# A decoder trunk on one Trainium2 core: the first stage written out in a fixed order, with column sums of squares on TensorE, weight folding on ScalarE and x loaded from two queues

## The chip, the cores and the metric

The kernel runs on one core of a Trainium2 chip. The core has five engines with a queue of instructions each: PE (TensorE, matrix products), ACT (ScalarE), DVE (VectorE), POOL (GpSimd) and SP (SyncE, which here only starts transfers). Each engine works through its own queue in order and waits at an instruction until what it needs is there. Transfers between the chip's memory and the core run on 16 DMA engines that are started from a queue.

The metric is the device time of one execution in microseconds (us), as the median of several runs. Times inside an execution are read from a profile of one execution, counted from the start of its span.

## What is computed

A trunk of two decoder layers over 1024 tokens of width 1024, all in float32. Cut to the part that matters here:

```python
h = x
for l in range(DEPTH):                       # 2 layers
    u = rmsnorm(h, attn_norm[l])             # u = h * rsqrt(mean(h*h) + eps) * g
    proj = u @ w_in[l]
    rq, rk, rv, rg, dq, dk, dv = jnp.split(proj, offsets, axis=-1)
    ret = retention_chunkwise(rq, rk, rv)    # 4 heads, gated by silu(rg)
    dif = diff_attention(dq, dk, dv, lam)    # 4 heads, two softmaxes subtracted, causal, ALiBi
    h = h + jnp.concatenate([ret, dif], -1) @ w_out[l]
    u = rmsnorm(h, ffn_norm[l])
    h = h + (jax.nn.silu(u @ w_gate[l]) * (u @ w_up[l])) @ w_down[l]
return rmsnorm(h, final_norm)
```

Only the beginning is touched by the change: the first `rmsnorm` on `x` and the first three products that follow it, which are `dk`, `dq` and `dv` of attention heads 0 and 1.

## The kernel before

The activations lie transposed: `h` is eight tiles `h[k]` of 128 channels x 1024 tokens, `k` = 0 to 7, and every step works on the two halves of 512 tokens. In the profile these tiles are called `a`. A product over the 1024 channels is a sum over `k` in one PSUM bank. To keep float32 precision at a higher rate, nearly every operand is split in two fp32r parts, `hi` (a cast on ACT) and `lo` (the difference, on DVE or POOL), and a product is three matmuls: hi times hi, hi times lo, lo times hi (`mm3`, and the same in `tm_pair`).

The first stage of the program, in the order in which `run` writes it:

- **Loads.** All from SP's queue: half of the first weight tile (`wr`), four `x` tiles of half 0, the other half of the weight, four more `x` tiles, the second weight tile (L1202, L1198), then the eight tiles of half 1, then two weight tiles for the values.
- **First products, early.** The K and Q products of head 0 for half 0 don't wait for the norm. The weights are multiplied by the norm's gains on DVE (L1205, into `fold`, called `sp` in the profile), plain float32 matmuls of the folded weights with raw `h` run on PE (`fm_first`, L289), and the result is scaled later by the norm's factor per token (L674).
- **Norm of half 0.** ACT squares each `h[k]` (L408), DVE adds the eight squares into `acc` (L415), PE sums `acc` over the channels with four tiny matmuls against a column of ones (L380, a *column sum*), a few 128x4 instructions on DVE and ACT turn this into the factor y (L385 to L392, L346, L389), and PE spreads y over the partitions by four transposes (L396). Then for each `k`: DVE multiplies `h[k]` by gain and y (L428), ACT casts it to `hi` (L430), and DVE, for two of the eight POOL, makes `lo` (L432).
- **Norm of half 1.** The same, with its squares and adds laid between the steps of half 0.
- **Values** of half 0 (`tm_pair`, L305 to L307): 96 matmuls of 128x256, then K, Q and values of half 1 (`fm_half`, L270 to L272, then L305 to L307), interleaved with the first attention scores (L556, L557).

What sets the order: for PE the order is as written, everywhere. For ACT, DVE, POOL and SP a scheduler orders the instructions by priorities, except in the feed-forward part, which is also written out by hand. `weave` interleaves two generators in a fixed proportion. Buffers come from pools of a fixed number of tiles (for example three `wr`, five `t`, two `kb`), and an instruction that writes a buffer waits until the last reader of its former content is done.

Of the kernel before, what the change touches and what calls it, by code (L numbers as in the profile page):

```python
# [146 lines left out]
class Trunk:  # L147
# [41 lines left out]
    def late_consts(self):  # L189
        nc, a = self.nc, self.a  # L190
        nc.sync.dma_start(self.tabs, a["tabs"])
# [92 lines left out]
    def fm_first(self, h, ws):  # L284

        for w in ws:
            ps = self.bank("mm")
            for k in range(KT):
                self.nc.tensor.matmul(ps, lhsT=w[:, P * k:P * k + P], rhs=h[k][:, 0:HT], start=k == 0,  # L289
                                      stop=k == KT - 1)  # L290
                yield 4
            self.first_ps.append(ps)

# [78 lines left out]

    def rsqrt_rows(self, parts, dim, cols=HT, gap=14):
        nc = self.nc
        nt = cols // P
        x = self.t("nx", 2, [P, 4])[:, :nt]
        banks = [self.bank(t) for t in (("s", "s", "t", "t")[:nt] if len(parts) > 1 else ("s",))]
        for i, sq in enumerate(parts):
            for t in range(nt):
                nc.tensor.matmul(banks[t % len(banks)][:, t:t + 1], lhsT=sq[:, P * t:P * t + P],  # L380
                                 rhs=self.ones[:, 0:1].bitcast(F32), start=i == 0, stop=i == len(parts) - 1)
# [11 lines left out]
        yield gap  # L393
# [4 lines left out]
        return out[:, :cols]  # L398

    def squares(self, h, sl, alone, kb=False, first=False):  # L400
# [4 lines left out]
        for k in range(KT):  # L405
            s = (tmp() if k else self.t("acc", 2, [P, 512]))[:, :n]
            with nullcontext() if first else self.tc.high_priority():
# [10 lines left out]
    def norm_half(self, h, hf, gcol, us, lag=11, gap=9, first=False, keep=False):  # L418
        nc = self.nc
        sl = slice(hf * HT, hf * HT + HT)  # L420
        parts = self.squares(h, sl, 0, True, first)
# [4 lines left out]
        for k in range(KT):  # L426
# [4 lines left out]
            eng = nc.gpsimd if keep and k in (1, 4) else nc.vector  # L431
            eng.tensor_tensor(out=lo[:, k], in0=f, in1=hi[:, k].bitcast(F32), op=ALU.subtract)  # L432
        if keep:
            self.first_y = self.big("sp")[:, 0:HT]
            nc.scalar.copy(self.first_y, y)
# [229 lines left out]
    def attention(self, l, us, w_first, norm1):  # L665
        wk, wq, wdv = w_first
        nc = self.nc
        v, qk, outs = {}, self.qk_tiles(), []
        kq = lambda hf: self.chain(self.stacks(wk, us, (hf,), qk[1], 1.0), self.stacks(wq, us, (hf,), qk[0], 0.125))
        first = [self.chain(kq(hf), self.values(wdv, us, hf, v)) for hf in range(NH)]  # L670
        if l == 0:
            for ps, st, scale in zip(self.first_ps, (qk[1], qk[0]), (1.0, 0.125)):
                f = self.tmp()
                nc.vector.tensor_tensor(out=f, in0=ps, in1=self.first_y, op=ALU.mult)  # L674
                self.stack(f, st, slice(0, HT), scale)
            self.weave(norm1, 40, self.values(wdv, us, 0, v), 48)
            self.late_consts()
        else:
            self.weave(norm1, 96, first[0], 96)
        self.prev, self.norms, self.outs = None, [], []  # L680
        for h in range(4):
# [7 lines left out]
            if h == 0:  # L689
                self.weave(self.att_part(l, A, 0, 4), PART0, first[1], 96)  # L690
# [416 lines left out]
    def layer(self, l, h, us, w_first, norm1, after):  # L1107
# [7 lines left out]
        o_out, rq, rk = self.attention(l, us, w_first, norm1)  # L1115
# [72 lines left out]
    def run(self):  # L1188
        nc = self.nc
        self.nf = 0  # L1190
        h = [self.big("a4") for _ in range(KT)]
        raws = [self.big("wr") for _ in range(2)]
        fold = [self.big("sp") for _ in range(2)]

        def load(hf, ks):
            sl = slice(hf * HT, hf * HT + HT)
            for k in ks:
                nc.sync.dma_start(h[k][:, sl], self.a["xT"][k][:, sl])  # L1198

        def load_w(i, c):  # L1200
            cs = slice(512 * c, 512 * c + 512)
            nc.sync.dma_start(raws[i][:, cs], self.a["wts"][i][:, cs])  # L1202
# [60 lines left out]
```

## Time and profile before

| what | value |
|---|---|
| median of 3 runs | 2310.18 us (2310.01, 2310.18, 2485.22) |
| profiled execution, its own time | 2310.15 us |
| span of the profiled execution | 2308.4 us |
| PE busy over the span | 2263.9 us (98%) |
| DVE, ACT, POOL busy | 1393.8, 1010.4, 762.4 us |
| first matmul of the first stage | 5.52 us |
| first matmul of half 1's K product | 46.30 us |
| first matmul of half 1's values | 59.60 us |

How to read it: the profiled execution's own time is 1.75 us above its span, and 0.03 us from the median. A busy PE is not a PE at its peak: the table of stretches has a column with the TensorE clock that was granted (1.00 is full speed), and the distance from the start of one matmul to the start of the next tells the real rate. A float32 matmul of 128x512 or 128x1 is recorded as two matmul instructions (called *passes* below), so the 16 matmuls of `fm_first` are 32 records.

### The profile page before, as it was taken

The page shows a single profiled execution, that of the slowest core. Times are in us where ns is not written, and L with a number is a line of the kernel's source. Part 1 is how long each engine was busy: PE and PEld are TensorE (multiplying, and loading weights), DVE is VectorE, ACT ScalarE, POOL GpSimd, SP SyncE. Part 2 cuts the span into 40 slices and gives each one's busy share as a digit, 9 for nine tenths or more (in the row PEclk, how much of TensorE's full clock was granted, in tenths as well). Part 3 has the DMA queues.
Part 4 walks back from the last instruction along what each step waited for, and adds up shares of the span by engine and source line. Part 5 has one row for each costly group of instructions (what it writes and reads, how often), then busy time and mean ns, then how long its engine had stood idle before and what let it go on. Part 6 is the DMA issues. An engine that isn't in the chain of part 4 may idle for free.

```text
span 2308.4 us, 30689 instructions
## 1 busy us (share of the span) xinstructions
PE 2263.9 (98%) x11328; PEld 1898.0 (82%) x11328; DVE 1393.8 (60%) x2576; ACT 1010.4 (44%) x1905; POOL 762.4 (33%) x608
## 2 busy tenths in 40 slices
PE   7999999999999999999999999999999999999998
PEld 5888898787788888888888888988878888888887
DVE  8777612987534333895567775059874443359856
ACT  5666533444333333543256665234443333344332
POOL 3111212122444455336121112211235444544350
PEclk9999999999999999999999999999999999999999
DMA  5212131111332322752232222112123232345422
GB/s 165 76 47 65 38 100 38 56 55 55 128 120 88 118 100 92 233 182 93 69 106 55 56 65 81 57 37 74 53 90 119 82 124 83 108 157 194 162 65 73
DMA packets 74214, 216.58 MB, mean 94 GB/s; under 512 B 8016, under 2 KB 10064, under 8 KB 74064
## 3 DMA queue, kind: packets, MB, share of 16 engines
q1 hardware_dynamic: 74064, 214.62, 28.8%
q8 instruction: 89, 1.46, 0.3%
q14 instruction: 61, 0.50, 0.1%
HBM read 162.16 MB, written 44.04 MB: 89 GB/s over the span
## 4 chain that ended last, share of the span: by engine, by line
PE 79%; DVE 11%; ACT 3%; issue 2%; DMA 2%; POOL 1%; DVEq 0%; SPq 0%; POOLq 0%; ACTq 0%
PE ps_mm L246 8%; PE ps_mm L247 7%; PE ps_mm L248 7%; PE ps_mm L271 6%; PE ps_mm L272 6%; PE ps_mm L270 6%; PE ps_s L246 4%; PE ps_s L247 4%; PE ps_s L248 4%; PE ps_t L246 3%; PE ps_t L247 3%; PE ps_t L248 3%; PE ps_mm L307 2%; PE ps_mm L305 2%; PE ps_mm L306 2%
## 5 line engine op out<-in xcount | busy, mean ns | idle before, releaser
L223 POOL TENSOR_TENSOR w<-wr,w 128x512 fp32r<-128x512 f32 x278 | 389.3, 1413 | 469.0 <-ACT w L222 433.9
L263 POOL TENSOR_TENSOR w<-wr,w 128x512 fp32r<-128x512 f32 x140 | 185.2, 1329 | 572.7 <-ACT w L262 537.6
L270 PE MATMUL ps_mm<-u,w 128*128 128x512 f32 (+1 forms) x735 | 296.0, 403 | 0.0
L271 PE MATMUL ps_mm<-u,w 128*128 128x512 f32 (+1 forms) x735 | 287.2, 391 | 2.0 <-DVE u L432 2.0
L272 PE MATMUL ps_mm<-u,w 128*128 128x512 f32 (+1 forms) x735 | 287.3, 391 | 0.0
L222 ACT CAST w<-wr 128x512 fp32r<-128x512 f32 x312 | 187.9, 619 | 142.3 <-DVE wr L889 86.5
L246 PE MATMUL ps_mm<-u,w 128*128 128x512 f32 x432 | 168.6, 390 | 0.0
L247 PE MATMUL ps_mm<-u,w 128*128 128x512 f32 x432 | 168.3, 390 | 0.0
L248 PE MATMUL ps_mm<-u,w 128*128 128x512 f32 x432 | 168.2, 389 | 0.0
L272 PEld LDWEIGHTS ps_mm<-u,w 128*128 128x128 f32 x735 | 138.0, 188 | 30.4
L271 PEld LDWEIGHTS ps_mm<-u,w 128*128 128x128 f32 x735 | 138.3, 188 | 26.1 <-DVE u L432 2.8
L270 PEld LDWEIGHTS ps_mm<-u,w 128*128 128x128 f32 x735 | 138.2, 188 | 23.9
L938 ACT COPY t<-ps_mm 128x512 f32<-128x512 f32 x76 | 44.7, 588 | 246.8 <-PE ps_mm L248 246.7
L262 ACT CAST w<-wr 128x512 fp32r<-128x512 f32 x140 | 85.7, 619 | 133.6 <-PE ps_mm L271 42.6
L305 PE MATMUL ps_mm<-w,u 128*128 128x256 f32 x448 | 128.5, 287 | 0.0
L306 PE MATMUL ps_mm<-w,u 128*128 128x256 f32 x448 | 127.7, 285 | 0.2 <-POOL w L263 0.2
L307 PE MATMUL ps_mm<-w,u 128*128 128x256 f32 x448 | 127.6, 285 | 0.0
L559 DVE CUSTOM_DVE_ANT_0 sp<-ps_s,wr 128x512 f32<-128x512 f32 (+2 forms) x192 | 103.2, 551 | 35.0 <-PE ps_s L557 33.8
L223 POOL TENSOR_TENSOR w<-t,w 128x512 fp32r<-128x512 f32 x52 | 74.9, 1440 | 146.6 <-ACT w L222 146.6
L563 ACT ACTIVATE sp<-sp,m 128x256 f32<-128x256 f32 (+7 forms) x128 | 99.1, 774 | 52.0 <-DVE m L562 51.3
L246 PE MATMUL ps_t<-u,w 128*128 128x512 f32 x288 | 114.0, 396 | 4.8 <-ACT t L938 4.8
L847 DVE TENSOR_TENSOR a<-a,ps_mm 128x512 f32<-128x512 f32 (+1 forms) x148 | 98.6, 666 | 33.1 <-PE ps_mm L248 19.5
(386 smaller groups left out, 5878.0 us busy)
## 6 DMA issues: line engine op xcount, KB each, us to landing
wr<-wts SPq DMA_DIRECT2D x190, 512.0 KB, 3.7
mx<-s_fast SPq DMA_DIRECT2D x56, 512.0 KB, 4.9
s_fast<-mx SPq DMA_DIRECT2D x48, 512.0 KB, 5.0
kb<-ka SPq DMA_DIRECT2D x64, 128.0 KB, 2.3
s_rest<-mx SPq DMA_DIRECT2D x12, 512.0 KB, 2.9
kb<-wts SPq DMA_DIRECT2D x12, 512.0 KB, 5.6
mx<-s_rest SPq DMA_DIRECT2D x12, 512.0 KB, 3.7
a<-xT SPq DMA_DIRECT2D x16, 256.0 KB, 5.4
```

The lines of the kernel that those rows point to most:

```text
L222: nc.scalar.copy(h, src)
L223: (eng or nc.gpsimd).tensor_tensor(out=o, in0=src, in1=h.bitcast(F32), op=ALU.subtract)
L246: mm(ps, lhsT=wh[:, c], rhs=bh, start=first and i == 0, stop=False, skip_group_check=True)
L247: mm(ps, lhsT=wh[:, c], rhs=bl, start=False, stop=False, skip_group_check=True)
L248: mm(ps, lhsT=wl[:, c], rhs=bh, start=False, stop=i == 3, skip_group_check=True)
L263: nc.gpsimd.tensor_tensor(out=o, in0=raw[:, cols], in1=h.bitcast(F32), op=ALU.subtract)
L270: mm(out, lhsT=lh, rhs=rh, start=first, stop=False)
L271: mm(out, lhsT=lh, rhs=rl, start=False, stop=False)
L272: mm(out, lhsT=ll, rhs=rh, start=False, stop=last)
L305: mm(o, lhsT=uh, rhs=wh, start=k == 0, stop=False)
L306: mm(o, lhsT=uh, rhs=wl, start=False, stop=False)
L307: mm(o, lhsT=ul, rhs=wh, start=False, stop=k == KT - 1)
```

## The change

The first stage becomes one function, `start`, whose instructions run on ACT, DVE, POOL and SP in the order in which they are written; the scheduler orders the rest of the program as before. Within it:

- `x` of half 0 comes from two queues: the odd `k` are started from ACT's queue, the even from SP's.
- The second weight tile (i = 1) is multiplied by the gains on ACT, in eight pieces of 128x128, instead of DVE.
- The squares of half 1 are not added up on DVE. Each goes to PE, where four column sums per square accumulate over the eight squares in four PSUM banks. They stand in PE's queue between the fourth and the fifth matmul of the Q product.
- The squares of half 1 and the splits of the value weights are laid between the steps of half 0's norm; the low parts of these weights move from POOL to DVE, two low parts of half 0's norm as well. The K weights' low parts stay on POOL, the Q weights' low parts go to DVE during the norm of half 1.
- The value weights are loaded into `mx` tiles instead of `wr`; `tabs` is loaded here.
- The values of half 0 are issued while the norm of half 1 is written, with all of the PE work of half 0 ahead of them.

```diff
+    def column_sums(self, banks, sq, nt, first, last):
+        for t in range(nt):
+            self.nc.tensor.matmul(banks[t % len(banks)][:, t:t + 1], lhsT=sq[:, P * t:P * t + P],
+                                  rhs=self.ones[:, 0:1].bitcast(F32), start=first, stop=last)
...
-        first = [self.chain(kq(hf), self.values(wdv, us, hf, v)) for hf in range(NH)]
-        if l == 0:
-            for ps, st, scale in zip(self.first_ps, (qk[1], qk[0]), (1.0, 0.125)):
-                f = self.tmp()
-                nc.vector.tensor_tensor(out=f, in0=ps, in1=self.first_y, op=ALU.mult)
-                self.stack(f, st, slice(0, HT), scale)
-            self.weave(norm1, 40, self.values(wdv, us, 0, v), 48)
+        part = lambda hf: self.chain(kq(hf), self.values(wdv, us, hf, v))
+        if begun:
             self.late_consts()
...
+    def start(self, us):
...
+        def fold_w(i, c):
+            if i == 0:
+                g = self.gains[:, 4 * c:4 * c + 4].rearrange("p (k o) -> p k o", o=1).broadcast_to([P, 4, P])
+                blocks = lambda t: halves(t)[c].rearrange("p (k m) -> p k m", m=P)
+                v(out=blocks(fold[i]), in0=blocks(raws[i]), in1=g, op=ALU.mult)
+                return
+            for k in range(4 * c, 4 * c + 4):
+                cs = slice(P * k, P * k + P)
+                nc.scalar.mul(fold[i][:, cs], raws[i][:, cs], self.gains[:, k:k + 1])
...
+        def norm(hf, y, n, beside=lambda k: None):
+            hi, lo = self.t("u", 4, [P, KT, HT], R32), self.t("u", 4, [P, KT, HT], R32)
+            us[hf] = (hi, lo)
+            fs = {}
+            for k in range(KT + 1):
+                if k < KT:
+                    fs[k] = self.tmp()
+                    mul(out=fs[k], in0=h[k][:, hf * HT:hf * HT + HT], scalar=self.gains[:, k:k + 1], in1=y,
+                        op0=ALU.mult, op1=ALU.mult)
+                    cast(hi[:, k], fs[k])
+                if k:
+                    low(lo[:, k - 1], fs.pop(k - 1), hi[:, k - 1])
+                beside(k)
...
+        load_w(0, 0)
+        for k in (1, 3, 5, 7):
+            load(0, k, nc.scalar)
+        load(0, 0)
+        load(0, 2)
+        load_w(0, 1)
+        load(0, 4)
+        load(0, 6)
+        load_w(1, 0)
+        load_w(1, 1)
+        for k in r:
+            load(1, k)
...
+        for k in r:
+            sq = room[k % 4] if k else acc
+            nc.scalar.activation(sq, h[k][:, 0:HT], AF.Square)
+            if k:
+                v(out=acc, in0=acc, in1=sq, op=ALU.add)
+            if k == 2:
+                fold_w(0, 1)
+            if k in (1, 4):
+                split(w_kq[0], raws[0], k // 4)(nc.gpsimd)
+            fm(0, k)
+
+        fold_w(1, 0)
+        bank = [self.bank("s")]
+        self.column_sums(bank, acc, 4, True, True)
+        y = self.rsqrt_small(bank, D, 4)
+        for k in range(4):
+            fm(1, k)
+        y = self.rows(y, 4)
...
+        def square(k):
+            nc.scalar.activation(parts[k], h[k][:, HT:T], AF.Square)
+            self.column_sums(banks, parts[k], 4, k == 0, k == KT - 1)
+        square(0)
...
+        norm(0, y, 0, beside0)
+        for k in range(4, KT):
+            fm(1, k)
+        y1 = self.rsqrt_small(banks, D, 4)
+        keep = self.big("sp")[:, 0:HT]
+        nc.scalar.copy(keep, y)
+        y1 = self.rows(y1, 4)
...
+        first(0)
+        values = self.values(wdv, us, 0, v0)
...
+        norm(1, y1, 1, beside1)
+        self.drain(values)
...
+        with self.tc.manual_schedule(engines={e.Activation, e.DVE, e.Pool, e.SP}):
+            h, w_first, begun = self.start(us)
```

Two places show what the new order is. The first is PE's queue behind the first eight matmuls. The names: `ps_mm` is the product's bank, `a` the raw x, `sp` a folded weight, `c_ones` the ones of a column sum, `c_ident` the identity of the transposes, `ny` the norm's factor. Before:

```order
L289 MATMUL ps_mm_127<-a_6_81,sp_86 128x512
L380 MATMUL ps_s_135<-c_ones,acc_104 128x1 x4
L289 MATMUL ps_mm_127<-a_7_82,sp_86 128x512
L289 MATMUL ps_mm_127<-a_8_83,sp_86 128x512
L289 MATMUL ps_mm_180<-a_1_76,sp_87 128x512
L289 MATMUL ps_mm_180<-a_2_77,sp_87 128x512
L396 MATMUL ps_s_183<-c_ident,ny_141 128x128 x4
L289 MATMUL ps_mm_180<-a_3_78,sp_87 128x512
...
L289 MATMUL ps_mm_180<-a_8_83,sp_87 128x512
L380 MATMUL ps_s_281<-c_ones,acc_155 128x1 x4
L305 MATMUL ps_mm_295<-w_248,u_188 128x256
```

And now (of the 32 column sums of half 1, four for each of the squares in `kb` and `v` tiles, the first and the last are shown):

```order
L364 MATMUL ps_s_157<-c_ones,acc_118 128x1 x4
L1210 MATMUL ps_mm_116<-a_1_78,sp_89 128x512
...
L1210 MATMUL ps_mm_116<-a_4_81,sp_89 128x512
L396 MATMUL ps_s_174<-c_ident,ny_164 128x128 x4
L364 MATMUL ps_s_183<-c_ones,kb_179 128x1
...
L364 MATMUL ps_o_186<-c_ones,v_182 128x1
L1210 MATMUL ps_mm_116<-a_5_82,sp_89 128x512
...
L1210 MATMUL ps_mm_116<-a_8_85,sp_89 128x512
L396 MATMUL ps_s_296<-c_ident,ny_288 128x128 x4
L294 MATMUL ps_mm_322<-w_244,u_194 128x256
```

Half 0's transposes (the first L396) stood behind ten of the sixteen long matmuls and now stand behind twelve; the column sums of half 1, the last four long matmuls and half 1's transposes all stand ahead of the first value matmul (L305, now L294), where before half 1's transposes stood in the middle of the values.

The second place is DVE's queue behind the transposes of half 0. The names: `t` and `u` are a step's product and its low part, `acc` the sum of squares, `w` a low part of a value weight. Before:

```order
L428 SCALAR_TENSOR_TENSOR t_37_190<-a_1_76,c_gains,ps_s_183 128x512
L415 TENSOR_TENSOR acc_155<-acc_155,kb_166 128x512
L428 SCALAR_TENSOR_TENSOR t_38_194<-a_2_77,c_gains,ps_s_183 128x512
L415 TENSOR_TENSOR acc_155<-acc_155,kb_169 128x512
L432 TENSOR_TENSOR u_189<-t_37_190,u_188 128x512
L415 TENSOR_TENSOR acc_155<-acc_155,kb_172 128x512
```

And now:

```order
L1225 SCALAR_TENSOR_TENSOR t_40_196<-a_1_78,c_gains,ps_s_174 128x512
L1225 SCALAR_TENSOR_TENSOR t_41_204<-a_2_79,c_gains,ps_s_174 128x512
L1216 TENSOR_TENSOR u_195<-t_40_196,u_194 128x512
L1225 SCALAR_TENSOR_TENSOR t_42_217<-a_3_80,c_gains,ps_s_174 128x512
L1216 TENSOR_TENSOR u_195<-t_41_204,u_194 128x512
...
L1216 TENSOR_TENSOR u_195<-t_44_235,u_194 128x512
L1216 TENSOR_TENSOR w_245<-mx_110,w_244 128x512
```

The adds of half 1's squares are gone from between the steps of half 0, and four low parts of value weights came in further down. Behind the first stage PE's queue is the same instruction for instruction, 10734 rows up to the end.

More of the change, by code (lines that the diff above doesn't have):

```diff
@@ L1 @@
 import math
[L2 removed]
+from contextlib import ExitStack
 import numpy as np
@@ L397, in rsqrt_rows, with squares @@
                                 identity=self.ident)
-        return out[:, :cols]
-    def squares(self, h, sl, alone, kb=False, first=False):
+        return out
+    def squares(self, h, sl, alone, kb=False):
         nc = self.nc
@@ new lines, in start @@
+        fold_w(0, 0)
+        acc = self.t("acc", 2, [P, 512])
+        room = [x for _ in range(2) for x in halves(self.big("ka"))]
+        for k in r:
[8 more added lines that the diff above has]
+            fm(0, k)
```

153 lines of the change are left out of this document (87 added, 66 removed).

## Prediction, made before the changed kernel was run

> **What bounds the kernel now.** The page first.
>
> ```profile
> span 2308.4 us, 30689 instructions
> PE 2263.9 (98%) x11328; PEld 1898.0 (82%) x11328; DVE 1393.8 (60%) x2576; ACT 1010.4 (44%) x1905; POOL 762.4 (33%) x608
> PE 79%; DVE 11%; ACT 3%; issue 2%; DMA 2%; POOL 1%; DVEq 0%; SPq 0%; POOLq 0%; ACTq 0%
> ```
>
> TensorE is busy 98% of the span and holds 79% of the chain that ended last. The change touches the first 60 us of it, 2.6%. Behind the first stage PE's queue is row for row the same, so I take one instant as the meeting point of both programs: M, the start of the first value matmul of half 1. What M gains or loses, the program gains or loses, unless something behind it had slack; with PE at 98% I assume none. PE's timeline before M:
>
> ```profile
> 37.68 0.41 PE L305 MATMUL ps_mm<-w,u 128*128 128x256 f32 x1
> 37.90 0.41 PE L306 MATMUL ps_mm<-w,u 128*128 128x256 f32 x1
> ...
> 38.67 0.60 PE L396 MATMUL ps_s<-c_ident,ny 128*128 128x128 f32 x4
> ...
> 46.06 0.28 PE L306 MATMUL ps_mm<-mx,u 128*128 128x256 f32 x1
> 46.18 0.28 PE L307 MATMUL ps_mm<-mx,u 128*128 128x256 f32 x1
> 46.30 0.40 PE L270 MATMUL ps_mm<-u,w 128*128 128x512 f32 x1
> ...
> 51.95 0.50 PE L271 MATMUL ps_mm<-u,w 128*128 128x512 f32 x1 [0.89 <-DVE u L432]
> ...
> 59.60 0.28 PE L305 MATMUL ps_mm<-w,u 128*128 128x256 f32 x1
> ```
>
> M is 59.60. From half 1's first matmul at 46.30 to M are 13.30 us with one wait of 0.89 for a low part of u, so 12.4 us without it. A value matmul comes every 0.22 us at 37.68 and every 0.12 us at 46.06: the same instruction at half and at full clock. Which stretches run at half clock the table of stretches tells (columns: length; busy us of PE, PE's weight loads, DVE, ACT, POOL; granted clock; DMA share; GB/s):
>
> ```profile
> 24.00:26.00 2.00, 0.90 (x3) 0.07 (x1) 2.00 (x4) 1.79 (x4) 2.00 (x1) 1.00 0.00 0
> 26.00:28.00 2.00, 1.23 (x10) 1.26 (x11) 2.00 (x3) 1.92 (x4) 2.00 (x3) 1.00 0.00 0
> 28.00:30.00 2.00, 1.78 (x9) 1.49 (x8) 2.00 (x4) 0.62 (x1) 2.00 (x2) 0.51 0.00 0
> ...
> 36.00:38.00 2.00, 2.00 (x11) 2.00 (x11) 1.90 (x5) 1.50 (x4) 0.00 (x0) 0.50 0.17 36
> 38.00:40.00 2.00, 2.00 (x18) 2.00 (x18) 1.12 (x5) 0.00 (x0) 0.00 (x0) 0.93 0.99 210
> ```
>
> The clock is halved from about 28 to 38. The cause is in PE's earlier timeline:
>
> ```profile
> 5.52 8.09 PE L289 MATMUL ps_mm<-a,sp 128*128 128x512 f32 x12 [5.52 <-DMA a<-xT]
> 14.53 1.05 PE L380 MATMUL ps_s<-c_ones,acc 128*128 128x1 f32 x8 [0.92 <-DVE acc L415]
> 15.45 3.68 PE L289 MATMUL ps_mm<-a,sp 128*128 128x512 f32 x8
> 19.12 0.62 PE L396 MATMUL ps_s<-c_ident,ny 128*128 128x128 f32 x4
> 19.58 5.32 PE L289 MATMUL ps_mm<-a,sp 128*128 128x512 f32 x12
> 26.77 1.02 PE L380 MATMUL ps_s<-c_ones,acc 128*128 128x1 f32 x8 [1.88 <-DVE acc L415]
> ```
>
> PE ran dense until 24.9, waited 1.88 us for half 1's sum of squares, did 1.02 us of column sums, and at 28 the clock fell. It came back at about 38.2, after work without a pause since this row (it waited for a low part that POOL made):
>
> ```profile
> 34.10 0.58 PE L307 MATMUL ps_mm<-mx,u 128*128 128x256 f32 x1 [2.32 <-POOL u L432]
> ```
>
> So the return took 4.1 us of dense work.
>
> **The change part by part.** *Half 0's factor.* Its transposes start at 19.12, behind 20 passes. They now stand behind 24, at 5.32/12 = 0.44 us each at full clock 1.8 us more; the wait of 0.92 us for the column sum goes, since two more products stand ahead of it: 19.12 + 1.8 - 0.9 = 20.0. Folding the second weight leaves DVE, where it made half 0's factor late:
>
> ```profile
> 14.39 3.44 DVE L1205 TENSOR_TENSOR sp<-wr,c_gains 128x512 f32<-128x512 f32 x2
> 17.76 0.15 DVE L385 TENSOR_SCALAR nx<-ps_s 128x4 f32<-128x4 f32 x1
> ...
> 39.31 2.07 DVE L428 SCALAR_TENSOR_TENSOR t<-a,c_gains,ps_s 128x512 f32<-128x512 f32 x3 [0.82 <-PE ps_s L396]
> ...
> 42.84 1.90 DVE L432 TENSOR_TENSOR u<-t,u 128x512 fp32r<-128x512 f32 x3
> ```
>
> The column sum was there at about 15.5 and DVE took it at 17.76, two us later. That gain is now covered by the four extra passes on PE: the factor is ready earlier, the transposes are not. If PE were ahead, the gain would show.
>
> *Half 0's steps on DVE.* First multiply 39.31 - 38.67 = 0.64 us after the start of the transposes: 20.6. Then eight multiplies at 2.07/3 = 0.69, and eight low parts and four low parts of value weights at 1.90/3 = 0.63: 13.1 us, until 33.7. POOL's two low parts are gone. ACT beside it:
>
> ```profile
> 18.29 1.13 ACT L408 ACTIVATE kb<-a 128x512 f32<-128x512 f32 x2
> ...
> 55.96 0.40 ACT L636 ACTIVATE sp<-sp,z 128x128 f32<-128x128 f32 x1
> ```
>
> 19 casts and squares at 1.13/2 = 0.57 and four weight pieces. ACT's multiply by a column per partition on 128x128 is in the trace (0.40), so the eight pieces cost 3.2 us, half of them here: 10.8 + 1.6 = 12.4 us, just under DVE's 13.1. The other half lies behind the squares of half 0, in ACT's time before the column sum. Both are hidden; uncovered, a piece would cost 0.4.
>
> *x from two queues.*
>
> ```profile
> 0.73 1.28 ACT L181 ACT_TABLE_LOAD   x1 [0.73 <-PEq L1253]
> ...
> 1.64 1.85 SPq L1198 DMA_DIRECT2D a<-xT  x4
> ...
> 5.41 0.63 ACT L408 ACTIVATE acc<-a 128x512 f32<-128x512 f32 x1 [0.66 <-DMA a<-xT]
> ...
> 9.07 0.34 PEld L289 LDWEIGHTS ps_mm<-a,sp 128*128 128x128 f32 x1 [0.52 <-issue]
> ...
> 9.92 0.34 PEld L289 LDWEIGHTS ps_mm<-a,sp 128*128 128x128 f32 x1 [0.52 <-issue]
> ```
>
> ```profile
> 3.00:4.00 1.00, 0.00 (x0) 0.00 (x0) 0.00 (x0) 0.00 (x0) 0.00 (x0) 1.00 1.00 287
> 10.00:11.00 1.00, 1.00 (x3) 0.48 (x2) 1.00 (x1) 0.81 (x2) 0.94 (x1) 1.00 1.05 399
> ```
>
> Starting four transfers costs a queue 1.85 us; ACT, free of its table load at 2.0, is through at 3.9, before its first square at 5.41. Nothing is queued behind it that is due sooner. The DMA engines are already full from 3 on (share 1.00 and 1.05), so two queues move no more bytes: 0. PE in any case takes 0.85 us a pass at the start (9.07 to 9.92), half its later rate, and is itself the limit there. A gain is possible only if the first tiles land earlier; I keep it for a rival.
>
> *Column sums of half 1.* A group of eight records (one square) costs PE about 1.0 us at full clock (26.77, 1.02), so eight cost 8 us, in the place of one. DVE loses seven adds for it. A new square is due every 0.69 + 0.63 = 1.32 us; the last one stands behind six steps (20.6 + 6 x 1.32 = 28.5), two weight low parts (1.3) and some three instructions of ACT (1.7), so it comes at about 31.5. At full clock PE would follow at 32.5. But PE's dense work ends at about 19.6, and from there on it makes 1.0 us of 128x1 matmuls in every 1.32 us, of the kind that did not hold the clock at 28. I take it that the clock falls, as before some 3 us after the dense work with slack for the phase, so at 23 to 24.6. Then a group takes 2.0 us, longer than the 1.32 between squares: groups four to eight, from 24.6 (20.6 + 3 x 1.32) on, 5 x 1.95 = 9.7, end at 34.3. No row shows a 128x1 group at half clock; its bounds are 1.0 (it keeps its time) and 2.0 (all of it scales, as 0.12 to 0.22 did for the values), and I take 1.95, nearest to the row that scales.
>
> *The last four products of Q* (8 passes) now stand behind these sums and ahead of half 1's transposes. At half clock 8 x 0.85 = 6.8 us; if 4.1 us of dense work bring the clock back as after 34.10, 4.1 us are 4.8 passes and the other 3.2 cost 0.44 each: 5.5 us, until 39.8. Half 1's factor is hidden under them: from column sum to transposes it took 19.12 - 17.76 = 1.36 us before, with three more 128x1 reads at 0.15 some 1.8, 34.3 + 1.8 = 36.1.
>
> *Then* four transposes 0.4 (40.2), 96 value matmuls at 0.12 (11.5: 51.7), and the 12.4 us up to M: 64.1. DVE's work for half 1 starts at 40.2 and is
>
> ```profile
> 35.12 1.27 DVE L674 TENSOR_TENSOR t<-ps_mm,sp 128x512 f32<-128x512 f32 x2
> ...
> 36.50 1.40 DVE L505 SCALAR_TENSOR_TENSOR ka<-t,ka 64x512 fp32r<-64x512 f32 x2
> ...
> 49.75 0.68 DVE L529 TENSOR_TENSOR v<-ps_mm,v 128x512 fp32r<-128x512 f32 x1
> ```
>
> eight multiplies and eight low parts (10.6), the scaling and stacking of Q (0.64 + 1.40; K's lie before the transposes), one value part (0.68), one Q weight part (0.63): 13.9 us, ready at 54.6. PE needs the last low part seven steps of 3 x 0.23 us after 51.7, at 56.5: no wait.
>
> M moves from 59.60 to 64.1, +4.5 us. On the profiled execution's own 2310.15 us (0.03 from the median) that is **2314.6 us**. Its own range, from the clock's return (2 us sooner or, with the first values at half clock, 3 us later): 2312.5 to 2317.5.
>
> [...] The row: 1.88 us of waiting and 1.02 us of column sums cost the clock at 28. [...]
>
> **The rivals.** *The clock holds* (0.25). PE's gaps between column sums are about 0.3 us, and whether the 1.02 us at 26.77 counted as work the trace can't say: for it, the 0.92 us wait before 14.53 did no harm. Column sums end at 32.5, the Q products at 32.5 + 3.5 = 36.0, the factor, behind DVE's 33.7 + 1.8 = 35.5, is just covered; transposes 36.4, values 47.9, M 60.3: +0.7, 2310.9 us. M gains nothing even so, since all 16 long matmuls and the sums now stand ahead of the values.
>
> *Early tiles* (0.10), the only way to a gain I find: x lands sooner, the full clock starts four passes earlier (4 x 0.41 = 1.6 us) and then holds. M 58.7, -0.9: 2309.2 us. Against it the full DMA engines.
>
> *The clock stays down through the values* (0.06), the slow end. If PE pauses for the factor or the transposes within its first 4 us of dense work, the return starts over: the Q products cost 1.3 more and 96 values 0.10 each more, 9.6: 2314.6 + 10.9 = 2325.5 us. It decides from where the factor comes later than the Q products' end; my sum has 36.1 against 39.8, so I give it little.
>
> *Nothing arrives* (in the chances of the clock holding): DVE and ACT get less work, but PE's order sets M, so no change.
>
> **How the numbers follow.** Half clock 0.58, clock holds 0.25, early tiles 0.10, stays down 0.06; 0.01 for the unforeseen. The range reaches from just under the early tiles' time, 2308.5, to the upper end of the likeliest case, 2317.5; it leaves out the slow end and part of the early tiles. Two per cent, about what a measurement of this kernel can tell from no change, is 46 us; no case comes near it, since the whole stage is 60 us: within 0.98, faster 0.01, slower 0.01.
>
> **What the new profile would show.** Half 0's transposes near 20 and its multiplies from about 20.6, back to back; a granted clock of 0.50 from 23 to 25 on until 38 to 39; column sums a group every 2.0 us, the fifth Q product at about 34; first value matmul at about 40, M at about 64. A clock of 1.00 between 24 and 36 would put M near 60 and prove me wrong on the main term; ACT still starting transfers after 5.4, DVE idle between half 0's multiplies, or a wait behind M that was not there before would break the sum in other places.

## The result and the profile after

The changed kernel takes 2336.42 us (median of 4 runs, 2336.15 to 2337.96), the kernel before, beside it, 2310.44 us (median of 4): a ratio of 1.0117, 95% interval 1.0105 to 1.0128. One of these four runs, 2485.22 us, was in a slow state and is left out of the ratio; the others took 2310.01 to 2310.71. The changed kernel is 26.0 us slower, where 2314.6 us and a range up to 2317.5 were forecast. The 2% of the prediction, 46 us, isn't reached.

The page of the changed kernel:

```profile
span 2334.4 us, 30787 instructions
PE 2293.5 (98%) x11384; PEld 1904.7 (82%) x11384; DVE 1385.7 (59%) x2578; ACT 1011.6 (43%) x1913; POOL 745.4 (32%) x600
```

TensorE is busy 29.6 us longer than before (2263.9): 8.1 us of it ahead of the meeting point M, 21.5 behind. PE's timeline up to the meeting point M:

```profile
7.95 9.61 PE L1210 MATMUL ps_mm<-a,sp 128*128 128x512 f32 x16 [7.95 <-DMA a<-xT]
...
21.72 0.60 PE L396 MATMUL ps_s<-c_ident,ny 128*128 128x128 f32 x4
...
24.35 0.38 PE L364 MATMUL ps_s<-c_ones,kb 128*128 128x1 f32 x2 [1.24 <-ACT kb L1284]
...
27.59 0.59 PE L364 MATMUL ps_s<-c_ones,kb 128*128 128x1 f32 x2 [1.16 <-ACT kb L1284]
...
29.32 0.56 PE L364 MATMUL ps_s<-c_ones,v 128*128 128x1 f32 x2
...
36.15 5.74 PE L1210 MATMUL ps_mm<-a,sp 128*128 128x512 f32 x8
41.72 0.60 PE L396 MATMUL ps_s<-c_ident,ny 128*128 128x128 f32 x4
42.08 0.36 PE L294 MATMUL ps_mm<-w,u 128*128 128x256 f32 x1
...
53.56 0.39 PE L269 MATMUL ps_mm<-u,w 128*128 128x512 f32 x1
...
60.28 0.51 PE L270 MATMUL ps_mm<-u,w 128*128 128x512 f32 x1 [0.98 <-DVE u L1216]
...
67.51 0.28 PE L294 MATMUL ps_mm<-w,u 128*128 128x256 f32 x1
```

M is 67.51, so the stage costs 7.9 us and not 4.5. The other 18 us come later. Pairing each PE instruction behind M with itself in the other trace gives the lag of the changed kernel along the program:

```
time before, us     68    351    634   1116   1477   1759   2200   2289
lag of after, us   7.9    7.9    9.2   16.2   16.4   18.2   25.4   26.0
```

There is no new wait: behind M TensorE was idle for 32.7 us before and is for 29.3 now. The lag stands still in some stretches and grows steadily in others, by 7 us from 634 to 1116. The table of stretches for one such piece, PE alone, before and then after (length, busy us, matmuls, granted clock, DMA share, GB/s):

```profile
640.00:720.00 80.00, 80.00 (x353) 1.00 0.34 114
```

```profile
640.00:720.00 80.00, 80.00 (x347) 1.00 0.29 99
```

Both are full and both at full clock, and one gets 353 matmuls through in 80 us where the other gets 347: on average a matmul takes 1.7% longer. From start to start, products of 128x512 were 227 or 226 ns apart in most cases before; now the most frequent distances are 229, 238 and 237 ns.

### The profile page after: what moved, and what is told of

It reads as the page before. It is cut to its first block, busy times and chain, and to the rows that moved or that the text cites. A ratio compares the mean times of both kernels' runs of the same rounds, so it can differ in the third digit from the quotient of the medians.

```text
span 2334.4 us, 30787 instructions
## 1 busy us (share of the span) xinstructions
PE 2293.5 (98%) x11384; PEld 1904.7 (82%) x11384; DVE 1385.7 (59%) x2578; ACT 1011.6 (43%) x1913; POOL 745.4 (32%) x600
## 4 chain that ended last, share of the span: by engine, by line
PE 83%; DVE 11%; ACT 3%; issue 1%; DMA 1%; POOL 0%; DVEq 0%; SPq 0%; ACTq 0%; POOLq 0%
PE ps_mm L245 8%; PE ps_mm L246 8%; PE ps_mm L247 8%; PE ps_mm L270 7%; PE ps_mm L269 6%; PE ps_mm L271 6%; PE ps_s L247 4%; PE ps_s L245 4%; PE ps_s L246 4%; PE ps_t L245 3%; PE ps_t L246 3%; PE ps_t L247 3%; PE ps_mm L296 2%; PE ps_mm L294 2%; PE ps_mm L295 2%
## 5 line engine op out<-in xcount | busy, mean ns | idle before, releaser
L222 POOL TENSOR_TENSOR w<-wr,w 128x512 fp32r<-128x512 f32 x278 | 386.9, 1404 | 479.2 <-ACT w L221 461.0
L262 POOL TENSOR_TENSOR w<-wr,w 128x512 fp32r<-128x512 f32 x134 | 175.3, 1315 | 568.1 <-ACT w L261 550.3
L245 PE MATMUL ps_mm<-u,w 128*128 128x512 f32 x432 | 170.9, 396 | 0.0
L247 PE MATMUL ps_mm<-u,w 128*128 128x512 f32 x432 | 170.6, 395 | 0.0
L246 PE MATMUL ps_mm<-u,w 128*128 128x512 f32 x432 | 170.4, 395 | 0.0
L294 PE MATMUL ps_mm<-w,u 128*128 128x256 f32 x448 | 127.3, 284 | 0.0
L838 DVE TENSOR_TENSOR a<-a,ps_mm 128x512 f32<-128x512 f32 (+1 forms) x148 | 98.6, 666 | 35.9 <-PE ps_mm L247 21.5
```

Source lines behind the costliest of these rows:

```text
L222: (eng or nc.gpsimd).tensor_tensor(out=o, in0=src, in1=h.bitcast(F32), op=ALU.subtract)
L245: mm(ps, lhsT=wh[:, c], rhs=bh, start=first and i == 0, stop=False, skip_group_check=True)
L246: mm(ps, lhsT=wh[:, c], rhs=bl, start=False, stop=False, skip_group_check=True)
L247: mm(ps, lhsT=wl[:, c], rhs=bh, start=False, stop=i == 3, skip_group_check=True)
L262: nc.gpsimd.tensor_tensor(out=o, in0=raw[:, cols], in1=h.bitcast(F32), op=ALU.subtract)
L294: mm(o, lhsT=uh, rhs=wh, start=k == 0, stop=False)
```

## The experiments

**Where the tiles lie.** Behind M the instructions of PE are the same, but their tiles are not where they were. The pools hand out addresses in the order in which the program first asks for each tag (the name of a kind of tile, such as `u` or `w`), and the new first stage asks in another order. This is the address in on-chip memory at which the tags begin, modulo 256 bytes (called its *phase* here), as the two programs assign it:

```
           sp   w    mx   ka   u    v    kb
before     96  224  224  224  224  224   96
after      96   96   96   96  224  224  224
```

What moved them is small: `nx` and `ny`, two tags of 64 bytes each, lie between `kb` and `u` before, and between `w` and `kb` after. Every large tile is a multiple of 2048 bytes, so only these 128 bytes shift the phase. Of a product's two operands, the row names the moving one first and the weights second (`u,w`). Sorted by the phase of the moving operand against that of the weights, the distances between products of 512 columns (fp32r, those of 218 to 245 ns, mean) are:

```
before   equal  (u, v, ka against w)      6373 products  227.6 ns
before   128    (sp against w)             787 products  232.6 ns
before   128    (kb against u)              96 products  232.9 ns
after    128    (u, v against w)          5596 products  232.8 ns
after    equal  (sp, ka against w)        1577 products  228.3 ns
after    equal  (kb against u)              96 products  227.0 ns
```

Each pair of this table that changed its phase changed its pace, in both directions. Small groups outside it don't sort so cleanly: before, `u` against `mx`, with equal phases, took 231.9 ns in 16 distances, and the scores (`ka` and `kb` against `a`, 118 distances) lie between 231 and 234 ns in both programs. In the whole program 6984 products of 512 columns have equal phases before and 1776 after. The six runs of this part change addresses alone: the instruction lists of all engines stay what they were.

Common to them is a function that asks for all buffers of the named tags at the start of `run`, without using them; an order of tags fixes the addresses. In the changed kernel with the order of the kernel before (run e1):

```diff
     def run(self):
         self.nf = 0
+        self.places("a4 wr sp acc kb nx ny u t2 w mx ka v")
```

> The changed kernel, every instruction as it was, with the tiles in on-chip memory put back where the kernel before has them. Theory of places (a 512-column product is slow, about 232.8 ns start to start, where the weights' address and the moving operand's address differ by 128 modulo 256, and fast, about 227 ns, where they are equal; the new first stage touches the pools in another order and so moves the tiles): the drift of about 18 us after the first stage goes, the first stage's own 7.9 us stay: 2318 us (2316 to 2320), most frequent distances 227 and 226 ns. Rival of the program (the longer instruction stream, the second DMA queue or the other order of the first stage slows what follows): no change, 2336 us (2334 to 2338), distances stay spread over 229 to 238 ns.

2317.69 us, ratio to the kernel before 1.0033 (1.0019 to 1.0046), as the theory had it. The same stretch has the old number of matmuls again:

```profile
640.00:720.00 80.00, 80.00 (x353) 1.00 0.33 112
```

M is at 66.66, 0.9 us sooner than in the changed kernel with the same instructions. The clock did that: half 0's transposes come at 21.30 and not at 21.72, and the last four Q products take 5.1 us in place of 5.6. The stretch from 38 to 40, first this run, then the changed kernel:

```profile
38.00:40.00 2.00, 2.00 (x5) 0.78 (x4) 1.37 (x2) 1.02 (x2) 0.00 (x0) 0.78 0.21 45
```

```profile
38.00:40.00 2.00, 2.00 (x4) 0.97 (x3) 1.27 (x3) 1.26 (x2) 0.00 (x0) 0.50 0.01 4
```

The clock fell at 25.2 here and at 26.6 there, and returned at 38.9 and 40.3. So M of a single execution moves by 0.9 us with no change to the stage, and differences of that size say nothing in what follows.

The reverse, in the kernel before (e2):

```diff
+        self.places("a4 wr sp mx acc ka w nx ny kb v u t2")
```

> The kernel before, every instruction as it was, with the tiles at the addresses that they have in the changed kernel. Theory of places: 5208 more of its 8032 products of 512 columns get unequal phases, so it loses the 18 us of drift without any change of its first stage: 2328 us (2325 to 2331), and its first value product of half 1 still begins at 59.6 us. Rival of the program: 2310 us (2309 to 2312).

2330.11 us, ratio 1.0087 (1.0070 to 1.0104): the kernel before, with nothing but its tiles moved, loses 20.3 us. Its M is 59.75, and its lag behind the unmoved kernel is 0.1 us at 86, 9.4 at 1129 and 19.6 at 2292.

```profile
640.00:720.00 80.00, 80.00 (x347) 1.00 0.32 110
```

With this the rival of the program falls: the loss goes with the addresses and not with the first stage, whose second queue and length are still there in the first run and absent in the second. Then all large tiles in one phase, in the changed kernel (e3) and in the kernel before (e4):

```diff
+        self.places("nx ny")
```

> The changed kernel with the two small tags nx and ny (128 bytes together) allocated first, so that all large tiles begin at the same address modulo 256; 7968 of 8032 products of 512 columns have equal phases (6984 in the kernel before, 1776 in the changed one). Theory of places: 2318 us less up to 984 x 5.4 ns = 5.3 us for the products that were slow in the kernel before too: 2315 us (2312 to 2318). Rival of the program: 2336 us. If the address counts in another way (the distance between two tiles, not the phase), 2318 us or anything above.

> The kernel before with nx and ny allocated first: 984 more of its products of 512 columns get equal phases. Theory of places: 2310.4 less 0 to 5.3 us, 2307 us (2305 to 2310), and the products with the tag sp as the moving operand go from 232.7 to 227 ns. Rival of the program: 2310.4 us, no change.

2312.82 us (1.0012, 1.0003 to 1.0021) and 2304.76 us (0.9977, 0.9967 to 0.9986). Products with `sp` go to 226.9 and 226.8 ns. So the kernel before had part of the same loss; its 2304.76 us lie just under the forecast range (2305 to 2310). Two runs ask what counts in the address: everything moved by 32 more bytes, to phase 0 (e8), and `w`, `mx`, `ka`, `v` moved by 64 against `u`, `sp`, `kb` (e11; a tag `pad` of 32 and of 64 bytes in the list).

```diff
+        self.places("nx ny pad")
```

> The kernel before with one phase for all large tiles (e4_before_one_phase, 2304.8 us, where that phase is 224 modulo 256), moved by 32 bytes, so that the phase is 0. If only the difference between the two operands counts, no change: 2304.8 us (2304 to 2306), products at 227 ns. [...]

```diff
+        self.places("nx ny a4 wr sp acc kb u t2 pad w")
```

> The kernel before with the weights (tags w, mx) 64 bytes away, modulo 256, from u, sp and kb, and in phase with ka and v. If a phase difference of 64 is as bad as one of 128: u with w at 232 to 233 ns and v, ka with w at 227, time about 2326 us. If only the bit of 128 bytes counts, all at 227 ns, 2305 us. If it lies between, 229 to 231 ns.

Phase 0: 2302.48 us (0.9970, 0.9958 to 0.9982), products of `u` with `w` at 227.4 ns against 227.5 in e4. The products are as fast as in e4, as the text had it; the time is 1.5 us under its range and 2.3 us under e4, but the intervals overlap (e4: 0.9967 to 0.9986), so a gain from the position itself isn't shown. It is the fastest kernel of this study. 64 bytes apart: 2327.89 us in one run, `u` and `sp` with `w` at 233.3 ns, `ka` with `w` at 228.4, `v` with `w` at 227.0. A distance of 64 cost as much here as one of 128 (232.8 ns in the table above):

```profile
640.00:720.00 80.00, 80.00 (x347) 1.00 0.31 108
```

**The first stage.** The runs from here on are changes of e3, the changed kernel in one phase (2312.8 us, M at 67.5), so that addresses play no part. First the loads back on one queue (e5):

```diff
-        for k in (1, 3, 5, 7):
-            load(0, k, nc.scalar)
-        load(0, 0)
-        load(0, 2)
+        for k in range(4):
+            load(0, k)
         load_w(0, 1)
-        load(0, 4)
-        load(0, 6)
+        for k in range(4, KT):
+            load(0, k)
```

> The changed kernel with one phase for all large tiles (as e3_after_one_phase, 2312.8 us), and the eight tiles of x's first half again loaded from SP's queue alone, in the order of the kernel before. Theory that the second queue made the start late: the first product comes at 5.5 us in place of 7.6, the transposes of half 0 at about 19.5 in place of 21.8, the meeting point M (the first value product of half 1, 67.5 us) at 65.2, the time 2310.5 us (2309.5 to 2311.5). Rival, that the last tile sets the end of the stage and both orders bring it at the same time: first product at 5.5, transposes unchanged within 0.5 us, time 2312.8 (2312 to 2313.5).

2310.22 us, ratio 1.0006 (0.9997 to 1.0015). The time is the one that the theory forecast, 2.6 us under e3, but the intervals overlap, so a gain isn't shown; M of the profiled execution, 67.15, is nearer to the rival's 67.5 than to the theory's 65.2, and that execution took 2313.23 us, 3 us above the median. PE's timeline, and the stretches (length; busy us of PE, its weight loads, DVE, ACT, POOL; granted clock; DMA share; GB/s):

```profile
5.26 9.63 PE L1210 MATMUL ps_mm<-a,sp 128*128 128x512 f32 x16 [5.26 <-DMA a<-xT]
16.00 1.05 PE L364 MATMUL ps_s<-c_ones,acc 128*128 128x1 f32 x8 [1.11 <-DVE acc L1263]
...
20.44 0.60 PE L396 MATMUL ps_s<-c_ident,ny 128*128 128x128 f32 x4
...
34.86 6.51 PE L1210 MATMUL ps_mm<-a,sp 128*128 128x512 f32 x8
41.20 0.60 PE L396 MATMUL ps_s<-c_ident,ny 128*128 128x128 f32 x4
```

```profile
22.00:24.00 2.00, 0.94 (x7) 0.94 (x7) 1.98 (x4) 2.00 (x5) 0.00 (x0) 0.87 0.84 335
24.00:26.00 2.00, 2.00 (x11) 2.00 (x11) 1.36 (x3) 2.00 (x7) 0.00 (x0) 0.50 0.05 20
```

The first product comes 2.4 us sooner than in e3, half 0's transposes 1.2, and so does the end of the column sums (34.86 against 36.04). The clock falls before 24 and not after 26, but it comes back no sooner (40.6 against 40.4), so the last four Q products take 6.3 us in place of 5.7, and of the lead 0.5 us is left at half 1's transposes (41.20 against 41.72).

Next the last four Q products between the column sums (e6), and both edits in one (e7):

```diff
             if k >= 5:
                 lows.pop(0)()
+            if 2 <= k < 6:
+                fm(1, k + 2)
         norm(0, y, 0, beside0)
-        for k in range(4, KT):
-            fm(1, k)
```

> As e3_after_one_phase, and the last four Q products stand between the groups of column sums (behind those of half 1's squares 3 to 6) and not behind all of them. Theory of the clock (the sums, which wait for ScalarE's squares, leave TensorE so empty that its clock falls, and half clock then sets the length of the sums): with the products between them the clock stays up, sums and products together end at about 34 us and not at 41.9, M comes at about 60 us, the time is 2305 us (2303 to 2308). Rival of mere filling (the clock falls all the same; the products only fill the waits before 27.6 us): M at 63.5 to 66 us, time 2310 us (2308.5 to 2311.5). Rival that something else meets there (DVE's steps): no change, 2312.8.

> Both of the foregoing in one: x's first half from one queue, and the Q products between the column sums. If both theories hold and add up, 2312.8 - 2.3 - 8 = 2302.5 us (2300 to 2306), below the kernel before (2310.4) and its one-phase form (2304.8). If the last step of DVE or ScalarE is what M waits for, the gains don't add: no earlier than the better of the two alone.

2315.20 us (1.0024, 1.0014 to 1.0035) with M at 70.97, and 2313.53 us (1.0019, 1.0009 to 1.0029) with M at 67.50. The first comes 3.5 us later at M than e3, which no text had; the second can't be told from e3, and only the last sentence of its text, that the gains don't add, held. PE's timeline of the first:

```profile
29.16 2.05 PE L1210 MATMUL ps_mm<-a,sp 128*128 128x512 f32 x2
...
45.61 0.41 PE L296 MATMUL ps_mm<-w,u 128*128 128x256 f32 x1
...
50.09 0.35 PE L296 MATMUL ps_mm<-mx,u 128*128 128x256 f32 x1
50.28 0.28 PE L294 MATMUL ps_mm<-w,u 128*128 128x256 f32 x1
```

A product whose record lasts 1.10 us at full clock (e9 at 24.97) takes 2.05 here, and the products strewn between column sums didn't bring the clock back: it is down until 50, through 24 values at 0.21 us. With eight passes in one piece behind the sums, as the change has them, it came back (at 40.3, 4.1 us behind their start). So the products were put earlier, ahead of the fall (e9), and then idle products were added (e10):

```diff
         fold_w(1, 0)
+        fold_w(1, 1)
...
-            if k == 1:
-                fold_w(1, 1)
+            if k < 4:
+                fm(1, k + 4)
...
-        for k in range(4, KT):
-            fm(1, k)
```

> As e3_after_one_phase (2312.8 us, M at 67.5), but ScalarE folds the second half of Q's weights before half 0's norm, and the last four Q products follow the first four groups of column sums, from 22 us on, ahead of the fall of the clock at 27.4 us and not behind it (in e6_q_between_sums they came behind it, and the clock stayed down until 50 us). Theory (TensorE is what the stage waits for, and what counts is how much of its work is done at half clock): transposes of half 1 at 36.5 to 38 in place of 41.9, some of the values at half clock, M at 63 to 65, time 2309 us (2307.5 to 2311). Rival (half 1's steps on DVE are the bound in any order, and they start only when the squares are done): M not before 66.5, 2312 us or more. Rival (the clock falls later but as long, and all values run cold, 96 at 0.21 us): M at 68 or later, 2313 to 2316 us.

```diff
             nc.scalar.activation(parts[k], h[k][:, HT:T], AF.Square)
+            if k > 3:
+                for _ in range(3):
+                    mm(idle, lhsT=self.ones, rhs=us[0][0][:, k - 4], start=True, stop=True)
```

> As e9_q_early, and three idle products of 512 columns, whose result nobody reads, stand ahead of each of the last four groups of column sums, so that TensorE has no empty stretch there. Theory of the clock: it stays up through sums and values; groups 0.9 us and not 1.7; transposes of half 1 at 36, values 0.12 us each, M at 61 to 62.5, time 2307 us (2305 to 2309). If the clock falls all the same, the idle products only add: 12 x 0.45 = 5.4 us at half clock, and the time is 2312 us or more.

2312.32 us (1.0011, 1.0002 to 1.0020) with M at 68.31, and 2314.94 us (1.0027, 1.0017 to 1.0036) with M at 68.41. In e9 the clock falls all the same, at about 26 (the products at 27.33, 30.75 and 34.16 take 2.06 us); M is where the last text had it, though only the first 15 values ran at half clock and not all 96. In e10 it falls too, at about 27, and comes back:

```profile
31.44 2.27 PE L1290 MATMUL ps_mm<-u,c_ones 128*128 128x512 f32 x3
...
37.03 0.95 PE L1290 MATMUL ps_mm<-u,c_ones 128*128 128x512 f32 x3
...
41.66 1.11 PE L396 MATMUL ps_s<-c_ident,ny 128*128 128x128 f32 x4 [1.31 <-DVE ny L389]
```

Three idle products take 2.27 us at 31 and 0.95 at 37, and the transposes are at half clock again after 1.31 us of waiting for the factor. With the clock up for the last groups, half 1's transposes still come at 41.7. That doesn't decide on the theory of the clock: the idle products themselves took 4.7 us from start to start (2.07, 1.10, 0.79, 0.78), and the factor, which the Q products no longer hide, 1.31. At last two parts of the change undone: half 1's squares added on DVE (e12), and the second weight folded on DVE (e13).

```diff
+            if 0 < k < KT:
+                v(out=acc1, in0=acc1, in1=parts[k], op=ALU.add)
...
+        banks = [self.bank("s")]
+        self.column_sums(banks, acc1, 4, True, True)
         y1 = self.rsqrt_small(banks, D, 4)
```

> As e3_after_one_phase (2312.8 us, M at 67.5), but half 1's squares are added on DVE into one tile, as in the kernel before, and one group of column sums stands behind the last Q products. Theory that the eight groups of column sums at half clock are what makes the new first stage long, and DVE has room: transposes of half 1 at 36 to 38, M at 62 to 63.5, time 2307 to 2309 us. Rival, that DVE is as full as TensorE there (13.3 us of half 0's steps from 22.4 on, and seven adds of 0.62 us: 40 us, then sums, factor, transposes at 42 to 43): M at 67.5 to 69, time 2312 to 2315 us.

```diff
-            if i == 0:
+            if i < 2:
                 g = self.gains[:, 4 * c:4 * c + 4].rearrange("p (k o) -> p k o", o=1).broadcast_to([P, 4, P])
```

> As e3_after_one_phase, but the second weight is multiplied by the norm weights on DVE, as in the kernel before (two operations of 1.72 us in place of eight pieces on ScalarE of 0.3 each). If ScalarE's pieces stand on the path (the trace of the changed kernel has them on its chain of waits from 25.33 to 26.50), the path gets 1.2 us shorter and DVE 1.7 us longer at the same place: M within 0.7 of 67.5, 2312 to 2313.5 us. If DVE sets the end, M 1.7 to 3.4 later, 2314.5 to 2316 us. If ScalarE alone did, M 66.3, 2311.6 us.

2312.48 us (1.0009, 1.0000 to 1.0019), M at 67.81; and 2311.09 us (1.0005, 0.9995 to 1.0014), M at 66.61. The first goes as its rival said, with transposes 1 us sooner. PE's timeline:

```profile
25.93 5.40 PE L1210 MATMUL ps_mm<-a,sp 128*128 128x512 f32 x8 [3.35 <-ACT sp L1207]
37.87 1.84 PE L364 MATMUL ps_s<-c_ones,acc 128*128 128x1 f32 x8 [6.54 <-DVE acc L1292]
41.13 1.09 PE L396 MATMUL ps_s<-c_ident,ny 128*128 128x128 f32 x4 [1.43 <-DVE ny L389]
```

Here TensorE waits 6.5 us for DVE and still gets to the transposes at about the same time. In the second, the wait of 1.16 us for a square is gone:

```profile
26.98 0.57 PE L364 MATMUL ps_s<-c_ones,kb 128*128 128x1 f32 x2
...
35.52 5.44 PE L1210 MATMUL ps_mm<-a,sp 128*128 128x512 f32 x8
```

From half 0's transposes (21.66) to the end of the column sums are 13.86 us, against 14.43 in the changed kernel and in e3 and 14.42 in e1. ScalarE's pieces were on the path up to there, for 0.6 us. M comes 0.9 us sooner than in e3, but no sooner than in e1, which has the pieces (66.66); a gain at M or in the time isn't shown.

## Why the prediction was wrong

Of the 26.0 us, 7.9 are the first stage (2317.69 less 2309.82, addresses as before; with all tiles in one phase, e3 less e4, it is 8.1) and some 18 the moved tiles; e2 gives 20 for these by itself.

**The step that failed** is in the first part: "What M gains or loses, the program gains or loses", on the ground that PE's queue behind the stage is row for row the same. The queue was the same; the pace of its rows was not. It was asked whether something behind M had slack, and not whether a matmul could last longer. No row of the profile before names an address, but the sign was there: that kernel had two paces for the same instruction, 227 ns with `u` and 233 with `sp`.

5208 products more in unequal phases at 5.4 ns (232.8 after less 227.4 in e8) would be 28 us; 18 to 20 came. The count fits where TensorE is hardly ever idle: from 634 to 1116 and from 1759 to 2200, 1237 and 1116 such products give 6.7 and 6.0 us, and 7.0 and 7.1 came. From 1116 to 1477 it would be 3.4 us and 0.2 came; what absorbs it there was not separated.

**The first stage: +7.9 for +4.5.** Of the 3.4 us that are missing, 1.9 are there at half 1's transposes (41.72 for 39.8) and 1.5 come behind the values. Its terms against the trace:

- *x from two queues*, taken at 0. The first product came at 7.95 in place of 5.52, and half 0's transposes at 21.72 for 20.0. ACT's queue, and then SP's:

```profile
0.76 1.84 ACTq L1194 DMA_DIRECT2D a<-xT  x4
```

```profile
1.19 0.42 SPq L1197 DMA_DIRECT2D wr<-wts  x1
1.65 0.90 SPq L1194 DMA_DIRECT2D a<-xT  x2
2.96 0.33 SPq L1197 DMA_DIRECT2D wr<-wts  x1
5.48 0.86 SPq L1194 DMA_DIRECT2D a<-xT  x2
```

  ACT starts its four transfers at 0.76, beside its table load and not behind it as the text had it, so `x1`, `x3`, `x5`, `x7` are under way before `x0`, for which the first product waits. The argument that full DMA engines move no more bytes held (from 3 to 8 us 298 GB/s before and 308 now); that they move other bytes first was left out. What the mistake cost at M, e5 doesn't settle: 0.3 us in the profiled executions, 2.6 between medians whose intervals overlap.
- *ScalarE's fold pieces*, called hidden. Four of them (25.24 to 26.50) delay a cast, for which DVE waits 0.64 us, and a square, and without them (e13) the column sums end 0.6 us sooner; at M that is not shown.
- *Column sums at half clock* was the likeliest case and happened: full clock up to 26, 0.50 from 28 on.

```profile
24.00:26.00 2.00, 1.65 (x14) 1.58 (x14) 2.00 (x4) 2.00 (x6) 0.00 (x0) 1.00 0.01 2
26.00:28.00 2.00, 0.84 (x6) 0.76 (x7) 1.36 (x3) 2.00 (x6) 0.00 (x0) 0.66 0.00 0
28.00:30.00 2.00, 2.00 (x11) 2.00 (x11) 2.00 (x4) 2.00 (x5) 0.00 (x0) 0.50 0.00 0
```

  The fall came at 26.6 and not at 23 to 24.6, and a group took 1.71 us (29.32 to 36.15, four groups) and not 1.95. The five slow groups begin at 27.59, not 24.6, and end at 36.15, not 34.3. Counted from half 0's transposes the misses cancelled, by luck: 14.4 us to the end of the sums, and 14.3 were forecast. The rival "the clock holds" is out. What makes the clock fall no run shows: TensorE's longest waits there were 1.24 us and, as the clock fell, 1.16, both shorter than the 1.88 that the prediction names. Nor does one show the "slack for the phase" in the text's 23 to 24.6: the long products ended at 21.9 (18.21 and 3.68) and the clock fell 4.7 us later, where before it was 3.1 (24.9 to 28.0). Whether column sums count as work, which the prediction left open, stays open. The early-tiles rival lets "the full clock" start four passes earlier; no run shows a clock that starts there: before, the granted clock reads 1.00 from 5 to 13 us, while the weight loads come 0.85 us apart from 7.36 to 10.77 and 0.43 apart from 12.17 to 12.60.
- *The last four products of Q*: 5.57 us (36.15 to 41.72), forecast 5.5, and 96 values 11.48, forecast 11.5. Both held, the first with the clock back 4.1 us behind their start, as forecast.
- *The 12.4 us up to M* became 13.95, with 0.98 us of waiting where "no wait" stood. DVE's queue:

```profile
55.44 0.69 DVE L1216 TENSOR_TENSOR u<-t,u 128x512 fp32r<-128x512 f32 x1
58.18 0.29 DVE L555 CUSTOM_DVE_ANT_0 sp<-ps_s,wr 128x128 f32<-128x128 f32 x1 [2.05 <-PE ps_s L553]
...
58.40 1.23 DVE L1216 TENSOR_TENSOR w<-wr,w 128x512 fp32r<-128x512 f32 x1
59.55 0.68 DVE L1216 TENSOR_TENSOR u<-t,u 128x512 fp32r<-128x512 f32 x1
```

  The size of DVE's work was nearly right (all but two steps done at 56.1; the forecast had all done at 54.6 from a start 2 us earlier, where its own terms, 40.2 and 13.9, give 54.1), but a step of the first attention head stands ahead of the last low part of `u`, and DVE waits 2.05 us at it for a score from PE.

No single part was found that makes the new stage long. From half 1's transposes to M were 20.9 us before (38.67 to 59.60) and are 25.8 now (41.72 to 67.51): before, 36 of the 96 values were done ahead of those transposes, now all stand behind them (36 at 0.12 are 4.3 of the 4.9 us). No variant with all values behind them brought M under 66.6, whichever engine carried the sums, the folding or the loads. That the values' place is the cause is read from the rows; moving the values ahead was not tried, so it stays open.

**The size of the chances.** That no case of the stage could reach 2% was right. But 2% is not what a measurement of this kernel can tell from no change, as the text had it: 1.2% came out with an interval of a tenth of a per cent to each side. That the rivals all lay within the first 60 us was the gap: nothing among them spoke of the other 2250.

## What to carry to other kernels

The new order of allocation changed the pace of instructions that it left as they were: products of `u` and `v` with `w` came 227.6 ns apart before and 232.8 after. When two programs run the same rows at the same clock and the lag between them grows steadily, count matmuls in equal stretches and compare the addresses of the operands before looking for a wait. Here it paid to allocate the tags that aren't multiples of 256 bytes first, so that all large tiles share one phase: 5 to 7 us in the kernel before (e4, e8), from the addresses alone.

A lead won at the start of a stage isn't a lead at its end: 2.4 us at the first product (e5) were 1.2 at half 0's transposes, since TensorE now waited 1.1 us for DVE's sum of squares, and 0.5 at half 1's, since the clock came back no sooner (40.6 against 40.4).

## What the runs showed of the hardware that was not expected

- In the long streams of the table above, products of 128x512 (fp32r) came 227 to 228 ns apart from start to start when the moving operand and the weights begin at the same address modulo 256 (before, after, e4, e8), and 233 ns when they are 128 (before, after) or 64 bytes apart (e11); other distances weren't tried. Whether two reads collide, and which (weights are loaded beside running products: PEld is busy 82% of the span beside PE's 98%), no run shows.
- Column sums (128x1) didn't bring TensorE's clock back in the changed kernel, even where PE was full of them: it made nothing else from 27.59 to 36.15, and the stretch from 28 to 30 above is busy for 2.00 us of 2.00 at 0.50.
- The dense work up to the clock's return was not of one length: 4.2 us before (34.10 to 38.28), 4.1 in the changed kernel (36.15 to 40.30), 3.2 in e1 with the same instructions (35.7 to 38.9) and 5.7 in e5 (34.86 to 40.6). The clock was down for 10.2 us before (from 28.04), 13.7 in the changed kernel (from 26.64) and 13.7 in e1 (from 25.2). What sets these moments no run shows.
- DVE's multiply of a 128x512 weight by the gains took 0.68 us with POOL at rest and 1.72 beside POOL. Before, the two at 14.39 took 3.44 us together; in e13, where POOL rests, the same two (17.09, 24.34) took 0.69 and 0.68; POOL's timeline of the kernel before, and DVE's of the changed kernel, where POOL rests at that time:

```profile
14.13 3.15 POOL L263 TENSOR_TENSOR w<-wr,w 128x512 fp32r<-128x512 f32 x2 [3.19 <-ACT w L262]
```

```profile
11.32 0.68 DVE L1203 TENSOR_TENSOR sp<-wr,c_gains 128x512 f32<-128x512 f32 x1
```
